# Side work around the seven-part products of an output projection: one VectorE operation per unit, and ScalarE in the making of the scale and bias rows

## The chip, the cores and the metric

The kernel runs on one core of a Trainium2 chip. The metric is the time of one execution on the device, in microseconds (us). The engines are TensorE (PE in the profile, with PEld for its weight loads), VectorE (DVE), ScalarE (ACT), GpSimd (POOL), and the queue of SyncE (SPq) that issues nearly all DMAs. Each engine executes its own list of instructions in order and waits at semaphores for the others.

## The reference, cut to what matters

One layer over 256 frames of width 4096: an input projection, two groups of heads (an attention with forgetting and a linear recurrence), a gate, an output projection, and a LayerNorm of the residual sum:

```python
h = jnp.concatenate([fox_out, rwkv_out], axis=-1) * jax.nn.silu(z.astype(f32))
out = jnp.einsum('bsc,cd->bsd', h.astype(x.dtype), w_out)          # (256, 4096) @ (4096, 4096)
x = _layernorm(ALPHA * x.astype(f32) + out.astype(f32), ln_gain, ln_bias, LN_EPS).astype(x.dtype)
```

Everything is float32. The change touches only the output projection and the preparation of the LayerNorm.

## The kernel before, in words

**Products in three parts.** A float32 operand goes through TensorE as a high part and a low part. ScalarE casts the high part (`split`, line 149), VectorE subtracts it from the operand for the low part (line 150), and TensorE runs three matmuls of 128x512 for each product: high by high, low by high, high by low. The third one is the first that needs VectorE's low part. The low parts stand in a ring of three tiles, the high parts in a ring of four: VectorE can begin a low part when TensorE is through with the tile three before it, ScalarE when it is through with the tile four before.

**The output projection.** The 4096 output columns are eight blocks of 512. `wo{b}_{q}` is the weight tile of block b and rows 256q to 256q+255, two contraction tiles of 128, so a plain tile (kind `n` of the plan) costs 12 matmuls. The two halves of the frames are `oacc_0` and `oacc_1`. The plan, a list of (kind, block, q), sets the order: blocks 0 and 1, then block 2 (q 6 to 11 first, then 0 to 5, then 12 to 15), then blocks 3 and 4 as a pair, then 5 and 6 as a pair, then block 7.

**Units of seven-part products.** In a pair, the rows of q 6 to 11 (`FEW`) go by a scheme with seven products in place of eight for a 2x2 block matrix. One such q is a unit. GpSimd makes four sums of weights (`combine`, kinds `t12` and `t34`, lines 307 to 311, four operations of 128x512 into the tiles `t`), and ScalarE and VectorE split the parts `e1` (1024 columns), `e2` (512 columns), `e3` and `e4` (1024 columns each, from GpSimd's sums). Two plain tiles of the pair are woven into each unit, so a unit is 21 matmuls of parts and 24 of plain tiles, and its six splits come in the order e1, plain, e2, e3, plain, e4.

**Recombined left factors.** The scheme needs sums of the left operand too. For each q in `FEW`, `combine_left` runs six GpSimd operations (lines 1020 to 1025, tile `sf`), and `split_left` splits them on ScalarE and VectorE (lines 1031 and 1032, tiles `sq` and `h`), and then starts the recombination for q+2. The six `split_left` are in the list `todo` when block 2 begins, and the first two recombinations are made ahead of it.

**Side work.** `todo` holds small jobs, and `drain(k)` issues the next k of them at a place of the plan: in block 2 one job at q 0, 1, 3, 5 and 13, in a pair two jobs at each of the first four plain tiles and at those behind the last unit, one at every other plain tile and one at each e4. When a block is complete its results are added into the residual `res` (`add`, lines 1085 and 1087), its statistics are taken (`stats`, BN_STATS, line 1076), and the residual is multiplied by the LayerNorm gain `lg` (`gain`, line 1099). In a pair the inner products are merged first (`merge`, lines 1046 and 1049).

**Scale and bias rows.** At its end the kernel applies the mean and the bias with a matmul against `rows`, six partitions by 4096 columns. `load_tok(b)` makes the part of block b: two DMAs into `rr`, a ScalarE cast to `rh` (line 974), a VectorE product by a constant column to `rt` (line 976), and a VectorE multiply-add into `rows` (line 977). `load_tok` is called once for each block, close to the place where the block begins; the tiles `rr`, `rh` and `rt` have one buffer each.

A scheduler turns this program into one list of instructions for each engine. It may move an instruction ahead of others whose inputs come later, except where `issue_after` or `keep_in_program_order` holds it.

## Time and profile before

| what | us |
|---|---|
| median of 3 runs | 1913.76 (1913.2 to 1914.81) |
| the profiled execution's own time | 1912.92 |
| its span, first to last instruction | 1911.1 |
| PE busy | 1898.2 (99%) |
| DVE busy | 1477.9 (77%) |
| ACT busy | 1009.1 (53%) |
| POOL busy | 404.9 (21%) |

The execution has 1.8 us around its span. The granted TensorE clock was 0.999 of full speed. Matmuls are pipelined in TensorE: the length of one in a row is not its cost; the distance between the starts of two neighbours is. A line number such as L150 is a line of the kernel before; behind the change, lines from 970 on stand 6 to 18 lines lower. In a row of the timeline stand the start, the length, engine, line, operation, out<-in (buffer numbers left out), sizes, and in brackets the idle time ahead of the instruction with what ended it.

### The profile page before, as it was taken

The page shows a single profiled execution, that of the slowest core. Times are in us where ns is not written, and L with a number is a line of the kernel's source. Part 1 is how long each engine was busy: PE and PEld are TensorE (multiplying, and loading weights), DVE is VectorE, ACT ScalarE, POOL GpSimd, SP SyncE. Part 2 cuts the span into 40 slices and gives each one's busy share as a digit, 9 for nine tenths or more (in the row PEclk, how much of TensorE's full clock was granted, in tenths as well). Part 3 has the DMA queues.
Part 4 walks back from the last instruction along what each step waited for, and adds up shares of the span by engine and source line. Part 5 has one row for each costly group of instructions (what it writes and reads, how often), then busy time and mean ns, then how long its engine had stood idle before and what let it go on. Part 6 is the DMA issues. An engine that isn't in the chain of part 4 may idle for free.

```text
span 1911.1 us, 28218 instructions
## 1 busy us (share of the span) xinstructions
PE 1898.2 (99%) x9757; PEld 1576.5 (82%) x9757; DVE 1477.9 (77%) x2417; ACT 1009.1 (53%) x1577; POOL 404.9 (21%) x549
## 2 busy tenths in 40 slices
PE   9999999999999999999999999999999999999998
PEld 9887888888888888888888888888888878877786
DVE  7578868776877687768776877787778775799996
ACT  6554555456545654465446554645464554455443
POOL 0022102200211021002200220022002213386530
PEclk9999999999999999999999999999999999999999
DMA  9668777876777678766876687668767976766665
GB/s 348 181 209 229 199 204 227 232 222 186 231 223 230 186 223 233 227 192 210 235 228 193 208 251 217 195 208 244 216 197 218 308 247 191 234 210 213 204 226 183
DMA packets 272324, 421.37 MB, mean 220 GB/s; under 512 B 142579, under 2 KB 171397, under 8 KB 272181
## 3 DMA queue, kind: packets, MB, share of 16 engines
q1 hardware_dynamic: 271892, 419.23, 72.7%
q8 instruction: 76, 1.25, 0.3%
q14 instruction: 68, 0.55, 0.1%
q10 hardware_dynamic: 288, 0.34, 0.1%
HBM read 389.86 MB, written 29.64 MB: 220 GB/s over the span
## 4 chain that ended last, share of the span: by engine, by line
PE 95%; DVE 2%; POOL 1%; DMA 1%; ACT 0%; issue 0%; SPq 0%; DVEq 0%; ACTq 0%; POOLq 0%
PE acc L155 24%; PE acc L157 24%; PE acc L156 24%; PE oacc L995 5%; PE oacc L992 5%; PE oacc L993 5%; PE rh L738 1%; PE gp L624 1%; PE up L769 1%; PE sp L779 1%; PE accl L157 0%; PE p L993 0%; PE accl L156 0%; PE p L995 0%; PE p L992 0%; PE accl L155 0%
## 5 line engine op out<-in xcount | busy, mean ns | idle before, releaser
L853 POOL COPY pT<-lg 32x96 f32<-32x96 f32 x128 | 57.1, 446 | 633.2 <-DVE lg L849 628.4
L661 POOL COPY BKt<-BK 32x192 f32<-32x192 f32 x128 | 73.7, 576 | 62.5 <-DVE BK L658 57.5
L694 DVE TENSOR_REDUCE xc<-prod 128x8 f32<-128x16 f32 (+30 forms) x248 | 72.7, 293 | 6.6
L691 DVE TENSOR_TENSOR prod<-Nb,xc 128x8 f32<-128x8 f32 (+30 forms) x248 | 72.3, 292 | 3.0
L150 DVE TENSOR_TENSOR w_0l<-w,w_0h 128x1024 fp32r<-128x1024 f32 x31 | 38.4, 1238 | 33.6 <-ACT w_0h L149 25.1
L149 ACT CAST w_0h<-w 128x1024 fp32r<-128x1024 f32 x31 | 32.5, 1048 | 54.9 <-DMA w<-in_w_main_dram 38.0
L149 ACT CAST w_8h<-w 128x1024 fp32r<-128x1024 f32 x31 | 32.6, 1052 | 48.7 <-PE acc L156 17.3
L149 ACT CAST w_6h<-w 128x1024 fp32r<-128x1024 f32 x31 | 32.7, 1055 | 46.9 <-PE acc L156 36.9
L150 DVE TENSOR_TENSOR w_9l<-w,w_9h 128x1024 fp32r<-128x1024 f32 x31 | 38.0, 1226 | 24.7 <-ACT w_9h L149 9.8
L150 DVE TENSOR_TENSOR w_11l<-w,w_11h 128x1024 fp32r<-128x1024 f32 x31 | 37.9, 1223 | 21.8 <-PE acc L157 16.1
L150 DVE TENSOR_TENSOR w_10l<-w,w_10h 128x1024 fp32r<-128x1024 f32 x31 | 37.9, 1223 | 20.4 <-issue 7.9
L150 DVE TENSOR_TENSOR w_15l<-w,w_15h 128x1024 fp32r<-128x1024 f32 x31 | 38.0, 1225 | 18.3 <-issue 12.9
L550 POOL COPY hr<-hr 32x16 f32<-32x16 f32 x64 | 45.7, 715 | 26.8 <-DVE hr L547 24.4
L150 DVE TENSOR_TENSOR w_6l<-w,w_6h 128x1024 fp32r<-128x1024 f32 x31 | 38.9, 1255 | 16.0 <-ACT hry L812 10.3
L149 ACT CAST w_10h<-w 128x1024 fp32r<-128x1024 f32 x31 | 32.6, 1053 | 34.0 <-DMA w<-in_w_main_dram 18.6
L149 ACT CAST w_1h<-w 128x1024 fp32r<-128x1024 f32 x31 | 32.7, 1053 | 33.9 <-DMA w<-in_w_main_dram 21.3
L155 PE MATMUL acc<-w_15h,x 128*128 128x512 f32 x124 | 50.2, 405 | 0.0
L155 PE MATMUL acc<-w_9h,x 128*128 128x512 f32 x124 | 50.0, 403 | 0.0
L157 PE MATMUL acc<-w_12l,x 128*128 128x512 f32 x124 | 48.5, 391 | 1.1 <-DVE w_12l L150 1.1
L150 DVE TENSOR_TENSOR w_7l<-w,w_7h 128x1024 fp32r<-128x1024 f32 x31 | 37.9, 1222 | 15.1 <-PE acc L157 13.1
L155 PE MATMUL acc<-w_14h,x 128*128 128x512 f32 x124 | 49.5, 399 | 0.0
L150 DVE TENSOR_TENSOR w_3l<-w,w_3h 128x1024 fp32r<-128x1024 f32 x31 | 37.8, 1221 | 14.9 <-PE acc L157 14.6
(1031 smaller groups left out, 6896.2 us busy)
## 6 DMA issues: line engine op xcount, KB each, us to landing
w<-in_w_main_dram SPq DMA_DIRECT2D x496, 512.0 KB, 4.1
wo<-in_w_o_dram SPq DMA_DIRECT2D x122, 512.0 KB, 4.6
bt<-bk SPq DMA_DIRECT2D x88, 128.0 KB, 4.2
Nb<-nd SPq DMA_DIRECT2D x16, 512.0 KB
hd<-hl SPq DMA_DIRECT2D x29, 256.0 KB
h<-hd SPq DMA_DIRECT2D x29, 256.0 KB, 6.2
wr<-in_w_first_dram SPq DMA_DIRECT2D x15, 384.0 KB, 6.8
lr<-in_w_lora_dram SPq DMA_DIRECT2D x15, 336.0 KB, 6.6
```

The source lines that it names most:

```text
L149: latest[1] = nc.scalar.copy(hi[:, :n], src[:, :n])
L150: latest[0] = nc.vector.tensor_tensor(lo[:, :n], src[:, :n], hi[:, :n].bitcast(F32), ALU.subtract)
L155: nc.tensor.matmul(acc[:, :n], xs[k][:, 0, tt], hi[:, o : o + n], start=(k == 0), stop=False)
L156: nc.tensor.matmul(acc[:, :n], xs[k][:, 1, tt], hi[:, o : o + n], start=False, stop=False)
L157: nc.tensor.matmul(acc[:, :n], xs[k][:, 0, tt], lo[:, o : o + n], start=False, stop=(k == KT - 1))
L661: nc.gpsimd.tensor_copy(BKt[B * b : B * (b + 1), :, :, B * a : B * (a + 1)], BK[B * a : B * (a + 1), :, : NCH - 1, B * b : B * (b + 1)])
L691: first = nc.vector.tensor_tensor(prod[:, :, :, s + 1 :], nb[:, :, s : s + 1, s + 1 :].to_broadcast([P, 2, NJ, w]), xc[:, :, :, s + 1 :], ...
L694: solved = nc.vector.tensor_reduce(xc[:, :, :, s : s + 1], prod[:, :, :, s:], AX.X, ALU.add)
L853: (nc.gpsimd.tensor_copy if b % 2 else nc.scalar.copy)(pT[B * b : B * (b + 1), :, B * a : B * (a + 1)], lg[B * a : B * (a + 1), :, B * b : ...
L992: nc.tensor.matmul(acc, h, hi, start=n[0] == n[1], stop=False)
L993: nc.tensor.matmul(acc, l, hi, start=False, stop=False)
L995: nc.tensor.matmul(acc, h, lo, start=False, stop=not n[0])
```

## The change

The row making leaves `load_tok` for a function of its own, `load_rows`, in which ScalarE makes `rt` as well as `rh`, tied behind the latest weight cast; the last step, into `rows`, becomes a job. For blocks 0 and 1 it is issued at the old place; those for blocks 2 to 7 are started in block 2, at every second tile, each put at the head of `todo`. Block 2's places for jobs become a table, `before_2`. In a pair, a unit gets one job, at its first plain tile, in place of up to three; the first two plain tiles of the first pair get none.

```diff
@@ load_tok
         nc.sync.dma_start(out=lgain[b], in_=lng[:, o].to_broadcast([P, OB]))
+        if b < 2:
+            load_rows(b)()
+
+    def load_rows(b):
+        o = slice(b * OB, (b + 1) * OB)
         rr = rpool.tile([6, OB], F32, tag="rr", name=f"rr{b}")
         nc.sync.dma_start(out=rr[0:3], in_=lng[:, o].to_broadcast([3, OB]))
         nc.sync.dma_start(out=rr[3:6], in_=lnb[:, o].to_broadcast([3, OB]))
         rh = rpool.tile([6, OB], F32R, tag="rh", name=f"rh{b}")
-        nc.scalar.copy(rh, rr)
         rt_ = rpool.tile([6, OB], F32, tag="rt", name=f"rt{b}")
-        nc.vector.tensor_scalar(rt_, rh.bitcast(F32), cs[0:6, C_ROW : C_ROW + 1], None, ALU.mult)
-        nc.vector.scalar_tensor_tensor(rows[0:6, o], rr, cs[0:6, C_ROW + 1 : C_ROW + 2], rt_, ALU.mult, ALU.add)
+        with tc.issue_after(latest[1].ins):
+            nc.scalar.copy(rh, rr)
+            nc.scalar.mul(rt_, rh.bitcast(F32), cs[0:6, C_ROW : C_ROW + 1])
+        return lambda: nc.vector.scalar_tensor_tensor(rows[0:6, o], rr, cs[0:6, C_ROW + 1 : C_ROW + 2], rt_, ALU.mult, ALU.add)
@@ before the loop over the plan
     count = {3: 0, 5: 0}
+    plan_2 = [q for _, b, q in plan if b == 2]
+    before_2 = {2: 1, 4: 1, 6: 1, 7: 1, 8: 2, 9: 1, 10: 1, 11: 1, 12: 1, 13: 1, 15: 1}
     whole = len(FEW) * 6 + LEAD
@@ in the loop
-            drain((2 if n <= LEAD or n > whole else 1) if kind == "n" else kind == "e4")
-        elif b > 1:
-            drain(2 if b == NB - 1 else q in (0, 1, 3, 5, 13))
+            apart_ = kind == "n" and (n <= LEAD or n > whole)
+            if apart_ and (pair > 3 or n > 2):
+                drain(1 if (pair, n) == (3, LEAD) else 2)
+            elif not apart_ and (n - LEAD) % 6 == 5:
+                drain(1)
+        elif b == NB - 1:
+            drain(2)
+        elif b == 2:
+            turn_ = plan_2.index(q)
+            if turn_ in before_2:
+                drain(before_2[turn_])
+            if turn_ % 2 == 0 and turn_ < 12:
+                todo.insert(0, load_rows(2 + turn_ // 2))
```

TensorE's list is the same before and after. VectorE's loses the eight `rt` products, ScalarE's gains them. What the scheduler makes of the rest is shown at three places.

**VectorE, second half of block 2.** `wo_5l` and the like are low parts of weight tiles, `sq` and `h` a recombined left factor, and a row that writes `rows` is the last step of the row making. Before:

```order
L150 TENSOR_TENSOR wo_12l<-wo_12_16061,wo_12h 128x1024
L976 TENSOR_SCALAR rt_16497<-rh_16495,cs 6x512
L977 SCALAR_TENSOR_TENSOR rows<-rr_16492,cs,rt_16497 6x512
L150 TENSOR_TENSOR wo_13l<-wo_13_16091,wo_13h 128x1024
L1032 TENSOR_TENSOR sq_16145<-sf_16042,sq_16145 128x384
L1032 TENSOR_TENSOR h_14895<-sf_16042,h_14895 128x128
L150 TENSOR_TENSOR wo_14l<-wo_14_16121,wo_14h 128x1024
L976 TENSOR_SCALAR rt_16993<-rh_16991,cs 6x512
L977 SCALAR_TENSOR_TENSOR rows<-rr_16988,cs,rt_16993 6x512
L150 TENSOR_TENSOR wo_15l<-wo_15_16139,wo_15h 128x1024
```

After:

```order
L150 TENSOR_TENSOR wo_5l<-wo_5_16050,wo_5h 128x1024
L983 SCALAR_TENSOR_TENSOR rows<-rr_16031,cs,rt_16035 6x512
L150 TENSOR_TENSOR wo_12l<-wo_12_16069,wo_12h 128x1024
L1038 TENSOR_TENSOR sq_16147<-sf_16080,sq_16147 128x384
L1038 TENSOR_TENSOR h_14854<-sf_16080,h_14854 128x128
L150 TENSOR_TENSOR wo_13l<-wo_13_16122,wo_13h 128x1024
L983 SCALAR_TENSOR_TENSOR rows<-rr_16099,cs,rt_16103 6x512
L150 TENSOR_TENSOR wo_14l<-wo_14_16141,wo_14h 128x1024
L1038 TENSOR_TENSOR sq_16203<-sf_16092,sq_16203 128x384
L1038 TENSOR_TENSOR h_14895<-sf_16092,h_14895 128x128
L150 TENSOR_TENSOR wo_15l<-wo_15_16178,wo_15h 128x1024
```

The `rows` steps stand at other tiles, and the split of the third recombined factor (its `h` is `h_14854`), which stood ahead of `wo_12l`, now stands behind it. Ahead of the rows shown, the first two splits moved from behind `wo_2l` and `wo_3l` to behind `wo_4l`, one after the other.

**ScalarE at the same place.** `rh` and `rt` are the first two steps of the row making. Before:

```order
L149 CAST wo_13h<-wo_13_16091 128x1024
L1031 CAST sq_16145<-sf_16042 128x384
L1031 CAST h_14895<-sf_16042 128x128
L974 CAST rh_16495<-rr_16492 6x512
L149 CAST wo_14h<-wo_14_16121 128x1024
L149 CAST wo_15h<-wo_15_16139 128x1024
```

After:

```order
L981 CAST rh_16034<-rr_16031 6x512
L1037 CAST sq_16147<-sf_16080 128x384
L982 ACTIVATE rt_16035<-rh_16034,cs 6x512
L1037 CAST h_14854<-sf_16080 128x128
L149 CAST wo_13h<-wo_13_16122 128x1024
L149 CAST wo_14h<-wo_14_16141 128x1024
L1037 CAST sq_16203<-sf_16092 128x384
L981 CAST rh_16102<-rr_16099 6x512
L1037 CAST h_14895<-sf_16092 128x128
L982 ACTIVATE rt_16103<-rh_16102,cs 6x512
L149 CAST wo_15h<-wo_15_16178 128x1024
```

An `rt` now stands behind an `sq`, the cast that waits for GpSimd's recombination, and the `rows` step of VectorE that uses it stands ahead of the next low part.

**VectorE in the first pair, from the second unit's first plain tile.** `e_3_8l` is a part of the third unit (q 8). Before:

```order
L150 TENSOR_TENSOR wo_1l<-wo_1_16430,wo_1h 128x1024
L150 TENSOR_TENSOR e_3_7l<-t_3_7_16407,e_3_7h 128x1024
L150 TENSOR_TENSOR e_3_8l<-wo_8_16426,e_3_8h 128x1024
```

After:

```order
L150 TENSOR_TENSOR wo_1l<-wo_1_16460,wo_1h 128x1024
L150 TENSOR_TENSOR e_3_7l<-t_3_7_16436,e_3_7h 128x1024
L150 TENSOR_TENSOR e_3_8l<-wo_8_16456,e_3_8h 128x1024
L1105 TENSOR_TENSOR res_15796<-res_15796,lg_16108 128x512
L150 TENSOR_TENSOR wo_12l<-wo_12_16472,wo_12h 128x1024
```

Before, the last side operation of the first pair's units stands in the first unit (two additions, two BN_STATS and two gains around q 6). Now the two additions and one BN_STATS stand there, the other BN_STATS in the second unit, and one gain each in the third and the fourth. In the second pair, the two gains that stood in the first unit and at the head of the second now stand in the third and the fourth.

## The prediction

> **What bounds the kernel now.** I read the page's head first.

> ```profile
> span 1911.1 us, 28218 instructions
> PE 1898.2 (99%) x9757; PEld 1576.5 (82%) x9757; DVE 1477.9 (77%) x2417; ACT 1009.1 (53%) x1577; POOL 404.9 (21%) x549
> ```

> TensorE is busy for 99% of the span and sets the end, and its list of matmuls does not change. So only the moments count in which it waits. The starts in its timeline show them:

> ```profile
> 1674.74 0.39 PE L992 MATMUL oacc<-wo_14h,h 128*128 128x512 f32 x1
> ...
> 1677.46 0.39 PE L992 MATMUL oacc<-wo_15h,hl 128*128 128x512 f32 x1
> 1677.68 0.39 PE L993 MATMUL oacc<-wo_15h,hl 128*128 128x512 f32 x1
> 1678.60 0.50 PE L995 MATMUL oacc<-wo_15l,hl 128*128 128x512 f32 x1 [0.53 <-DVE wo_15l L150]
> ...
> 1691.88 0.39 PE L992 MATMUL p<-e_6h,h 128*128 128x512 f32 x1
> ...
> 1747.98 0.50 PE L995 MATMUL oacc<-wo_15l,hl 128*128 128x512 f32 x1
> ...
> 1778.36 0.39 PE L992 MATMUL p<-e_6h,h 128*128 128x512 f32 x1
> ...
> 1833.74 0.50 PE L995 MATMUL oacc<-wo_15l,hl 128*128 128x512 f32 x1
> ```

> A tile of 12 matmuls takes 1677.46-1674.74 = 2.72, so the pitch is 0.227. The step of 0.92 before 1678.60 has 0.7 of waiting in it, and 0.1 more in refilling: block 2 loses 0.8. From the first part of the first unit to the waiting matmul of the last there are five units of 45 and eight more, 233 matmuls or 52.8. The first pair took 56.1 (loses 3.3), the second 55.4 (loses 2.6). That is 6.7 us to be had in all, 0.35%.

> Why the units lose shows in VectorE's and GpSimd's timelines of one unit:

> ```profile
> 1713.53 2.32 DVE L150 TENSOR_TENSOR wo_12l<-wo,wo_12h 128x1024 fp32r<-128x1024 f32 x1
> 1715.78 1.78 DVE L150 TENSOR_TENSOR e_8l<-res,e_8h 128x512 fp32r<-128x512 f32 x1
> ...
> 1718.61 1.21 DVE L150 TENSOR_TENSOR wo_2l<-wo,wo_2h 128x1024 fp32r<-128x1024 f32 x1
> ...
> 1724.23 2.32 DVE L150 TENSOR_TENSOR wo_13l<-wo,wo_13h 128x1024 fp32r<-128x1024 f32 x1
> 1723.18 2.28 POOL L310 TENSOR_TENSOR t<-wo 128x512 f32<-128x512 f32 x1
> 1700.00:1750.00 50.00, 49.60 (x213) 39.24 (x212) 50.00 (x29) 26.72 (x28) 40.33 (x19) 1.00 0.55 195
> ```

> The same split takes 1.21 (start to start 1.14) or 2.32: beside a GpSimd operation VectorE stands still for 1.1. The last row is the table of stretches (length; busy PE, PEld, DVE, ACT, POOL): VectorE is busy for all 50 us. A unit costs it five splits of 1.14, one of 0.6 and four holds of 1.1 = 10.7, as wo_12l to wo_13l shows; TensorE needs 45x0.227 = 10.2. So a unit loses 0.5 **with no side operation at all**, and the third to the sixth had none.

> What a side operation costs beside GpSimd:

> ```profile
> 1688.47 3.46 POOL L310 TENSOR_TENSOR t<-res,res 128x512 f32<-128x512 f32 x1
> 1690.27 0.68 DVE L1076 BATCH_NORM_STATS2 lst<-res 128x6 f32<-128x512 f32 x1
> 1690.88 1.60 DVE L1099 TENSOR_TENSOR res<-res,lg 128x512 f32<-128x512 f32 x1
> ```

> BN_STATS takes its usual 0.68 while GpSimd's operation runs, and fits inside a hold. The gain waits until that operation ends: it costs 0.6 of its own and admits a hold of 1.1 ahead of the split behind it. [...]

> **First term: block 2's start, +0.3** (0 to +0.7).

> ```profile
> 1641.11 1.22 DVE L150 TENSOR_TENSOR wo_8l<-wo,wo_8h 128x1024 fp32r<-128x1024 f32 x1
> 1642.51 0.40 PE L995 MATMUL oacc<-wo_8l,h 128*128 128x512 f32 x1
> L977 DVE SCALAR_TENSOR_TENSOR rows<-rr,cs,rt x8: 723/798/1112, 1623.0 to 1688.5; 6x512 fp32r<-6x512 f32 x8
> L976 DVE TENSOR_SCALAR rt<-rh,cs x8: 468/733/1055, 1622.5 to 1685.3; 6x512 f32<-6x512 f32 x8
> ```

> wo_8l is ready 0.18 ahead of its matmul. Block 1's `rows` step (at least 0.72) now stands behind wo_7l; in exchange rt and rows leave the place ahead of block 0's additions, but these can move forward only to where TensorE is done with block 0, some 0.3. 0.7-0.3-0.18 = 0.2, with the refill 0.3.

> **Second term: the loop of four engines in block 2, +1.0** (-0.8 to +3.1). Eight rt products of about 0.73 (5.9 us) leave VectorE; ScalarE gets them for about the 0.62 of its `rh` below, hidden, as it is busy for 27 of 50 in the stretch above. That is not the price. The price is what `rows` now waits for:

> ```profile
> 1655.21 0.74 POOL L1020 TENSOR_TENSOR sf<-h 128x256 f32<-128x256 f32 x1 [28.60 <-DVE h L1032]
> 1662.96 0.74 POOL L1020 TENSOR_TENSOR sf<-h 128x256 f32<-128x256 f32 x1
> 1667.65 0.74 POOL L1020 TENSOR_TENSOR sf<-h 128x256 f32<-128x256 f32 x1
> 1670.18 3.73 POOL L1023 TENSOR_TENSOR sf<-sf 128x128 f32<-128x128 f32 x1
> 1674.40 0.74 POOL L1020 TENSOR_TENSOR sf<-h 128x256 f32<-128x256 f32 x1
> 1680.76 0.53 POOL L1025 TENSOR_TENSOR sf<-sf 128x128 f32<-128x128 f32 x1
> 1659.11 1.21 DVE L150 TENSOR_TENSOR wo_4l<-wo,wo_4h 128x1024 fp32r<-128x1024 f32 x1
> 1669.81 0.83 DVE L977 SCALAR_TENSOR_TENSOR rows<-rr,cs,rt 6x512 fp32r<-6x512 f32 x1
> 1670.57 1.20 DVE L150 TENSOR_TENSOR wo_13l<-wo,wo_13h 128x1024 fp32r<-128x1024 f32 x1
> 1672.38 1.21 DVE L150 TENSOR_TENSOR wo_14l<-wo,wo_14h 128x1024 fp32r<-128x1024 f32 x1
> 1674.47 0.52 ACT L1031 CAST sq<-sf 128x384 fp32r<-128x384 f32 x1 [3.61 <-POOL sf L1025]
> 1675.09 0.62 ACT L974 CAST rh<-rr 6x512 fp32r<-6x512 f32 x1
> 1675.74 0.80 DVE L976 TENSOR_SCALAR rt<-rh,cs 6x512 f32<-6x512 f32 x1 [2.16 <-ACT rh L974]
> 1677.34 1.21 DVE L150 TENSOR_TENSOR wo_15l<-wo,wo_15h 128x1024 fp32r<-128x1024 f32 x1
> ```

> GpSimd makes four recombinations without a break, in 7.8, 4.7, 6.8 and 6.9. The second has 4.7; the third lost 3.3 to one operation of some 0.4 that began beside `rows` (1670.18) and came to an end only behind wo_14l, when VectorE fell idle: VectorE's run shuts GpSimd out. Behind a recombination stand, in a line, ScalarE's sq, then rh, then VectorE's rt, rows and the low part of the next tile: from 1674.40 to 1678.55, 4.1 us. That is the 0.8 lost in block 2 today.

> Now the first recombination begins behind wo_4l instead of wo_2l: two tiles or 5.4 later, at 1660.6. The first takes about 4.9, since VectorE falls idle behind wo_5l (its `rows` waits for this very recombination): 1665.5. The second meets `rows`, wo_12l, sq, h, wo_13l in a run and is shut out: 7, 1672.5. Behind it stand sq, rh, h, rt on ScalarE, then rows and wo_14l on VectorE, 4.1 by the line above: 1676.6. TensorE needs wo_14l at 1674.74+0.45 = 1675.2: loss 1.4. The third is shut out again, until 1679.5; then sq and h (0.8), the cast of wo_0 (1.05) and its low part (1.2): 1682.5, where TensorE, late by 1.4, needs it at 1682.0: 0.4 more. The fourth finds slack. Loss 1.8 for 0.8: +1.0. I take this middle as it uses each row at its nearest place. Low end: no loss (-0.8). High end: the four as slow as before on average, 26.1 in all, which puts wo_2l, behind the fourth, at 1660.6+26.1+3.3 = 1690.0, needed at 1677.46+3x2.72+0.45 = 1686.1: loss 3.9.

> **Third term: the units of the first pair, -0.7** (-1.8 to +0.3).

> ```profile
> 1794.08 1.54 DVE L150 TENSOR_TENSOR wo_1l<-wo,wo_1h 128x1024 fp32r<-128x1024 f32 x1 [0.97 <-issue]
> 1798.91 2.32 DVE L150 TENSOR_TENSOR wo_12l<-wo,wo_12h 128x1024 fp32r<-128x1024 f32 x1
> ```

> Five side operations in and just ahead of the first unit are gone (rt, rows, a BN_STATS, two gains). So VectorE enters the second unit with the ring full, and begins the second plain tile there (wo_1l) when TensorE leaves wo_5, some 0.2 behind it. From wo_1l's start to wo_12l's end are 7.15 in the second pair. The new gain ahead of wo_12l adds 0.6 and lets a hold of 1.1 in: 8.85. TensorE needs wo_12l 35 matmuls or 7.9 after leaving wo_5: 8.85+0.2-7.9, or 1.2, lost. The next unit, again with a gain, costs 11.3 against 10.2: 1.1, with slips 1.3. In the fifth the hold, which the gain had moved ahead, is not paid twice, and in the sixth 0.1 is lost. Together 2.6 for 3.3. Ends: VectorE arrives late as before (+0.3), or half of the holds fall into its idle time as one does ahead of wo_1l (1.5 lost, -1.8).

> **Fourth term: the second pair, 0** (-1.1 to +0.3). The gain that stood ahead of wo_5l and lost about 1 there is gone, but the same 2.6 comes back behind the two later gains. Work on VectorE that is only moved within a saturated stretch ends at the same moment.

> At nothing I cost: the 16 small DMAs of `rr`, which are as many as before and stand in SPq among weight loads that already wait for `rows` without TensorE waiting (row below); the later loads of `lg`, half a pair ahead of use; and the end, where the same instructions come in a slightly other order and VectorE has about 2 us in hand.

> ```profile
> SPq L971 <- DVE rows L977: 10.7, 5, 3.9
> ```

> **Sum**: +0.3+1.0-0.7+0 = +0.6. The profiled execution's 1912.92 becomes 1913.5; it stands 0.84 below the median of the runs, so against the median 1914.4.

> **Rivals.** (1) *GpSimd is not shut out*: it keeps its turn, recombinations take 4.7 each, the second ends at 1670.0, wo_14l is ready in time, block 2 loses nothing; with the pairs at their low ends (1.5 lost in each) the sum is +0.3-0.8-1.8-1.1 = -3.4, 1910.4. For it: the second recombination, and GpSimd's regular turns in the units. Against: 1670.18 and two more like it. [...] The row shows the waiting operation passed over by four.
> (2) *The loop closes*: slower. With recombinations of 6.5 on average the second term is +3.1 and the sum +2.7; from 6.8 on it passes +3.8; at 7.8, the worst row, wo_2l is ready at 1695.1, 9.0 late, and the sum is +7.8: 1921.6. For it: three of four rows were 6.8 or more. Against: `rows` stands beside two of the four now, and VectorE has gaps.
> (3) *The change doesn't do what it says*: units 5 and 6 have no side operation and two others a gain that is no cheaper than before, so units gain nothing: +1.3, 1915.1. This lies in my range.

> **Chances.** Forecast with its neighbourhood (-1.5 to +2.6) and rival 3: 0.60; rival 1: 0.22, half of it beyond -0.2%; rival 2: 0.18, 0.14 of it beyond +0.2%. A measurement of this kernel tells about 0.2% (3.8 us) from no change. So faster 0.11, within 0.75, slower 0.14. The range reaches into both rivals: 1910.8 to 1918.0.

> **What would show it.** Right: TensorE waits at wo_14l and wo_0l of block 2, behind VectorE idle for ScalarE's rt, behind sq for GpSimd; waits of about 1 at wo_12l and wo_13l of each pair; none at wo_0l and wo_5l there. Wrong: 233 matmuls of a pair in under 54.5 us, or recombinations above 6.8.

## The result, and the profile after

| kernel | median us (runs) | lowest to highest | ratio to before, 95% interval |
|---|---|---|---|
| before | 1913.33 (22) | 1911.98 to 1914.81 | |
| changed | 1916.81 (22) | 1915.50 to 1918.19 | 1.0019, 1.0012 to 1.0025 |

The change makes the kernel slower, by 3.5 us. The forecast was 1914.4, a sum of +0.6 on the profiled execution. The direction and the range hold, the size doesn't. The head of the profile after reads as before, with 0.9 us more of TensorE and 9 us less of VectorE:

```profile
span 1915.6 us, 28227 instructions
PE 1899.1 (99%) x9757; PEld 1579.4 (82%) x9757; DVE 1468.6 (77%) x2409; ACT 1013.7 (53%) x1585; POOL 390.8 (20%) x549
```

The changed kernel's TensorE timeline, at the places that the prediction counts (start, length, operation, idle time ahead of it and what ended it):

```profile
1676.38 0.50 PE L1001 MATMUL oacc<-wo_14l,h 128*128 128x512 f32 x1 [0.20 <-DVE wo_14l L150]
...
1682.35 0.50 PE L1001 MATMUL oacc<-wo_0l,h 128*128 128x512 f32 x1 [0.23 <-DVE wo_0l L150]
...
1689.32 0.50 PE L1001 MATMUL oacc<-wo_2l,h 128*128 128x512 f32 x1 [1.24 <-DVE wo_2l L150]
...
1694.46 0.39 PE L998 MATMUL p<-e_6h,h 128*128 128x512 f32 x1
...
1751.60 0.44 PE L1001 MATMUL oacc<-wo_15l,hl 128*128 128x512 f32 x1
...
1781.93 0.39 PE L998 MATMUL p<-e_6h,h 128*128 128x512 f32 x1
...
1805.80 0.50 PE L1001 MATMUL oacc<-wo_12l,h 128*128 128x512 f32 x1 [1.29 <-DVE wo_12l L150]
...
1817.35 0.50 PE L1001 MATMUL oacc<-wo_13l,h 128*128 128x512 f32 x1 [0.93 <-DVE wo_13l L150]
...
1838.17 0.50 PE L1001 MATMUL oacc<-wo_15l,hl 128*128 128x512 f32 x1
```

With the prediction's measure, time between two starts less 0.2267 for each matmul, three stretches can be compared: block 2 (216 matmuls, from wo_8's first to the first part of the pair), and 233 matmuls of each pair. The same table takes in the experiments below; where a kernel ran beside the kernel before on the same chip, the last column is its median less that one's.

| kernel | block 2 | first pair | second pair | sum | sum less before | median less before |
|---|---|---|---|---|---|---|
| before | 0.9 | 3.3 | 2.6 | 6.7 | | |
| changed | 2.6 | 4.3 | 3.4 | 10.3 | +3.6 | +3.5 |
| changed, run again | 2.6 | 4.3 | 3.4 | 10.3 | +3.6 | +3.5 |
| block-2 half alone | 2.6 | 1.9 | 2.4 | 6.9 | +0.2 | +0.4 |
| pair half alone | 1.2 | 3.9 | 3.8 | 8.9 | +2.2 | +1.8 |
| BN_STATS for gains | 2.6 | 2.0 | 1.5 | 6.1 | -0.6 | -0.6 |
| rows apart | 0.0 | 3.7 | 3.8 | 7.4 | +0.7 | +1.1 |
| no jobs in units | 0.0 | 2.0 | 1.5 | 3.4 | -3.3 | -0.7 |
| rows apart, old pairs | 0.0 | 1.5 | 2.5 | 4.0 | -2.7 | -1.9 |
| the same again | 0.0 | 1.5 | 2.5 | 4.0 | -2.7 | -2.0 |
| last gain behind | 0.0 | 1.5 | 1.5 | 3.0 | -3.7 | -2.7 |

The sum of the three stretches (+3.6) and the medians (+3.5) agree, so the changed kernel's loss is in these stretches. The two traced spans differ by 4.5. The other 0.9 stands ahead of block 2, which begins at 1642.9 in the changed kernel's trace and at 1642.1 in that of the kernel before, and anywhere from 1641.8 to 1643.7 in the traces of the experiments (but the one that adds long reductions).

**Block 2** waits at wo_14l and wo_0l, as the prediction says, but most of it at wo_2l. The chain there, from the timelines of VectorE, ScalarE and GpSimd (L983 writes `rows`, L982 makes `rt`, L1037 and L1038 are `sq` and `h`, L1026 to L1031 the recombination):

```profile
1668.54 3.87 POOL L1031 TENSOR_TENSOR sf<-sf 128x128 f32<-128x128 f32 x1
1672.45 0.52 ACT L1037 CAST sq<-sf 128x384 fp32r<-128x384 f32 x1 [1.98 <-POOL sf L1031]
1673.59 0.72 ACT L982 ACTIVATE rt<-rh,cs 6x512 f32<-6x512 f32 x1
1674.34 0.85 DVE L983 SCALAR_TENSOR_TENSOR rows<-rr,cs,rt 6x512 fp32r<-6x512 f32 x1 [2.25 <-ACT rt L982]
1674.73 3.73 POOL L1029 TENSOR_TENSOR sf<-sf 128x128 f32<-128x128 f32 x1
1685.11 1.29 POOL L307 TENSOR_TENSOR t<-res,wo 128x512 f32<-128x512 f32 x1
1685.17 0.52 ACT L1037 CAST sq<-sf 128x384 fp32r<-128x384 f32 x1 [2.39 <-POOL sf L1031]
1685.72 1.09 DVE L1038 TENSOR_TENSOR sq<-sf,sq 128x384 fp32r<-128x384 f32 x1 [0.91 <-ACT sq L1037]
1686.74 1.39 DVE L1038 TENSOR_TENSOR h<-sf,h 128x128 fp32r<-128x128 f32 x1
1688.05 1.21 DVE L150 TENSOR_TENSOR wo_2l<-wo,wo_2h 128x1024 fp32r<-128x1024 f32 x1
```

VectorE stands idle for `rt`, which stands behind `sq` on ScalarE, which waits for GpSimd, where the last operation of the recombination took 3.87; others of its shape take 0.46. Then VectorE's next run keeps another of them from ending for 3.73. The last recombination ends at 1685.1, and behind it stand the cast of wo_2 on ScalarE and `sq` and `h` on VectorE. These two, 0.54 and 0.27 at 1676.3, take 1.09 and 1.39 there, beside the sums of the first unit, which GpSimd began at 1685.1.

**The first pair** loses 1.9 at wo_12l, behind a gain, and then something that no line of the program contains. (By the condition `(n - LEAD) % 6 == 5` the job of a unit is issued at the unit's second plain tile, not at its first; in VectorE's list it lands ahead of the next unit's first plain tile.) The first five rows are VectorE and GpSimd, the others TensorE, then the table of stretches (length; busy PE, PEld, DVE, ACT, POOL; granted clock; DMA share and rate):

```profile
1712.65 2.31 DVE L150 TENSOR_TENSOR e_8l<-wo,e_8h 128x1024 fp32r<-128x1024 f32 x1
1714.89 1.78 DVE L1105 TENSOR_TENSOR res<-res,lg 128x512 f32<-128x512 f32 x1
1716.59 2.30 DVE L150 TENSOR_TENSOR wo_12l<-wo,wo_12h 128x1024 fp32r<-128x1024 f32 x1
1713.84 2.28 POOL L310 TENSOR_TENSOR t<-res,res 128x512 f32<-128x512 f32 x1
1716.08 1.73 POOL L311 TENSOR_TENSOR t<-wo,t 128x512 f32<-128x512 f32 x1
1718.94 0.50 PE L1001 MATMUL oacc<-wo_12l,h 128*128 128x512 f32 x1 [1.78 <-DVE wo_12l L150]
1719.98 0.53 PE L998 MATMUL oacc<-wo_12h,h 128*128 128x512 f32 x1
...
1723.28 0.49 PE L1001 MATMUL oacc<-e_8l,sq 128*128 128x512 f32 x1
1716.69:1720.10 3.41, 1.63 (x8) 1.03 (x7) 3.41 (x3) 1.04 (x1) 1.12 (x1) 1.00 0.67 163
1720.10:1723.51 3.41, 3.41 (x10) 2.67 (x9) 1.31 (x2) 1.04 (x1) 2.55 (x2) 0.50 0.79 289
```

From 1719.98 on, one microsecond after the wait is over, the matmuls' starts stand 0.32 apart once and then 0.42 to 0.43, in place of 0.227, for 3.3 us in all, and the granted clock is 0.50. The eight steps from 1719.98 to 1723.28 take 3.30 for 1.81, so 1.5 are lost there. Busy time doesn't show it: PE is busy for all of that last stretch.

### The profile page after: what moved, and what is told of

Read it like the earlier page. It is cut to its first block, busy times and chain, and to the rows that moved or that the text cites. A ratio compares the mean times of both kernels' runs of the same rounds, so it can differ in the third digit from the quotient of the medians.

```text
span 1915.6 us, 28227 instructions
## 1 busy us (share of the span) xinstructions
PE 1899.1 (99%) x9757; PEld 1579.4 (82%) x9757; DVE 1468.6 (77%) x2409; ACT 1013.7 (53%) x1585; POOL 390.8 (20%) x549
## 4 chain that ended last, share of the span: by engine, by line
PE 95%; DVE 2%; POOL 1%; DMA 0%; ACT 0%; issue 0%; SPq 0%; DVEq 0%; ACTq 0%; POOLq 0%
PE acc L155 24%; PE acc L157 24%; PE acc L156 23%; PE oacc L1001 5%; PE oacc L998 5%; PE oacc L999 5%; PE rh L738 1%; PE gp L624 1%; PE up L769 1%; PE p L999 1%; PE p L1001 1%; PE p L998 1%; PE sp L779 1%; PE accl L155 1%; PE accl L156 1%; PE accl L157 1%
## 5 line engine op out<-in xcount | busy, mean ns | idle before, releaser
L150 DVE TENSOR_TENSOR w_0l<-w,w_0h 128x1024 fp32r<-128x1024 f32 x31 | 38.2, 1231 | 32.3 <-ACT w_0h L149 24.2
L149 ACT CAST w_6h<-w 128x1024 fp32r<-128x1024 f32 x31 | 32.7, 1055 | 46.8 <-PE acc L156 36.8
L150 DVE TENSOR_TENSOR w_9l<-w,w_9h 128x1024 fp32r<-128x1024 f32 x31 | 38.0, 1226 | 24.8 <-ACT w_9h L149 12.7
L150 DVE TENSOR_TENSOR w_10l<-w,w_10h 128x1024 fp32r<-128x1024 f32 x31 | 37.9, 1224 | 22.9 <-ACT w_10h L149 8.8
L150 DVE TENSOR_TENSOR w_11l<-w,w_11h 128x1024 fp32r<-128x1024 f32 x31 | 37.9, 1222 | 20.7 <-PE acc L157 14.6
L150 DVE TENSOR_TENSOR w_6l<-w,w_6h 128x1024 fp32r<-128x1024 f32 x31 | 39.9, 1288 | 16.0 <-ACT hry L812 10.3
L150 DVE TENSOR_TENSOR w_15l<-w,w_15h 128x1024 fp32r<-128x1024 f32 x31 | 38.0, 1227 | 16.9 <-issue 15.4
L150 DVE TENSOR_TENSOR w_7l<-w,w_7h 128x1024 fp32r<-128x1024 f32 x31 | 37.9, 1222 | 15.1 <-PE acc L157 13.1
L150 DVE TENSOR_TENSOR w_3l<-w,w_3h 128x1024 fp32r<-128x1024 f32 x31 | 37.8, 1220 | 14.9 <-PE acc L157 14.6
L155 PE MATMUL acc<-w_1h,x 128*128 128x512 f32 x124 | 49.2, 397 | 0.0
```

Source lines behind the costliest of these rows:

```text
L149: latest[1] = nc.scalar.copy(hi[:, :n], src[:, :n])
L150: latest[0] = nc.vector.tensor_tensor(lo[:, :n], src[:, :n], hi[:, :n].bitcast(F32), ALU.subtract)
L155: nc.tensor.matmul(acc[:, :n], xs[k][:, 0, tt], hi[:, o : o + n], start=(k == 0), stop=False)
```

## The experiments

The first theory: two separable parts, block 2's loop (1.7 by the table) and the gains in the third and fourth unit (the rest, with the half clock in it). The rivals: one part alone is the cause; any operation in a unit costs alike; the half clock is chance.

### The block-2 half alone

The changed kernel, with the pairs' job places of before.

```diff
-            apart_ = kind == "n" and (n <= LEAD or n > whole)
-            if apart_ and (pair > 3 or n > 2):
-                drain(1 if (pair, n) == (3, LEAD) else 2)
-            elif not apart_ and (n - LEAD) % 6 == 5:
-                drain(1)
+            drain((2 if n <= LEAD or n > whole else 1) if kind == "n" else kind == "e4")
```

> The block-2 half of the change alone: row making by ScalarE and the table of places of block 2 stay, the pairs get the job places of the kernel before. Theory (two separable parts: the loop of four engines in block 2 costs 1.8 us, the gains in the third and fourth unit cost the rest): 1913.3 + 1.8 = 1915.1, with block 2 losing about 2.6 at wo_14l, wo_0l and wo_2l, and no half clock in the first pair, since no TensorE wait there exceeds 1.3. Rival A (the pairs alone make it slower; what block 2 loses is given back by the lead that the pair then has): 1913.3 to 1913.8. Rival B (block 2 is the whole cause, also of the pair's losses): 1916.8, with the waits at wo_12l of the first pair still there.

Measured: 1913.69, ratio 1.0003 (0.9994 to 1.0012). Rival A's time: block 2 loses its 2.6, and the first pair gives 1.3 of the 1.7 back. The rows of VectorE and GpSimd at the pair's start show by what:

```profile
1693.51 1.28 DVE L1105 TENSOR_TENSOR res<-res,lg 128x512 f32<-128x512 f32 x2
...
1690.06 2.38 POOL L311 TENSOR_TENSOR t<-wo,t 128x512 f32<-128x512 f32 x1
1697.80 1.29 POOL L307 TENSOR_TENSOR t<-wo,wo 128x512 f32<-128x512 f32 x1 [5.37 <-DVE e_6l L150]
```

VectorE, late by block 2's waits, comes to block 2's two gains at 1693.51, when GpSimd has ended its first sums (1690.06 + 2.38) and has not begun the next (1697.80). Both together take 1.28. In the kernel before they stand beside GpSimd and take 1.60 and 1.77. So the two parts aren't separable, and the part that writes the rows costs almost nothing by itself: alone the two halves lose 0.2 and 2.2 by the sums of the table, together 3.6.

### The pair half alone

The kernel before, with the changed pairs; the split that block 2 of the kernel before leaves over goes to the pair's first tile.

```diff
-            drain((2 if n <= LEAD or n > whole else 1) if kind == "n" else kind == "e4")
+            apart_ = kind == "n" and (n <= LEAD or n > whole)
+            if apart_ and (pair > 3 or n > 2):
+                drain(1 if (pair, n) == (3, LEAD) else 2)
+            elif apart_ and n == 1:
+                drain(1)
+            elif not apart_ and (n - LEAD) % 6 == 5:
+                drain(1)
```

> The pair half alone: block 2 and the row making as before, the pairs with one job per unit (the sixth recombined factor's split, which block 2 of the kernel before leaves over, is issued at the first tile of the first pair). Theory: waits of 1 to 2 us at wo_12l of both pairs behind the gain ahead of it, about 1 at wo_13l; +0.3 by waits in the first pair, +0.8 in the second, and 1.5 more if the wait at wo_12l is again long enough to halve the clock: 1914.4 without, 1915.9 with it. Rival A (pairs alone are the cause): 1916.8. Rival B (block 2 is the whole cause): 1912.6 to 1913.3, since two gains leave the first unit.

Measured: 1915.06, ratio 1.0010 (1.0002 to 1.0019). Slower by itself, without a half clock in its trace, and between what the theory (1914.4) and Rival A (1916.8) gave; Rival B (1912.6 to 1913.3) falls. The pairs lose 0.6 and 1.2 more than before. Block 2, which this kernel leaves as it was, loses 0.4 more in this trace, at wo_8l, which was ready only 0.18 ahead in the kernel before. The gain and its wait in the first pair:

```profile
1713.97 1.79 DVE L1099 TENSOR_TENSOR res<-res,lg 128x512 f32<-128x512 f32 x1
...
1718.04 0.50 PE L995 MATMUL oacc<-wo_12l,h 128*128 128x512 f32 x1 [1.55 <-DVE wo_12l L150]
1729.61 0.50 PE L995 MATMUL oacc<-wo_13l,h 128*128 128x512 f32 x1 [0.97 <-DVE wo_13l L150]
```

Here both waits come, at wo_12l and at wo_13l. In the changed kernel wo_13l is ready 0.25 ahead, because VectorE gained time while TensorE ran at half clock. So of the 1.5 that the half clock takes, about 1.1 stands in place of the wait at wo_13l.

### BN_STATS in place of the gains

The changed kernel, with one more BN_STATS of the same tile wherever a gain stands in a unit; these four multiplications are left out.

```diff
+        if in_unit:
+            return stats(m, b)
         nc.vector.tensor_tensor(res[m][:, o], ..., lgain[b], ALU.mult)
...
+                in_unit = True
                 drain(1)
+                in_unit = False
```

> The changed kernel in which each gain inside a unit (two in each pair) is replaced by one more BN_STATS of the same tile; these four multiplications by the gain are left out. Theory (an operation with two SBUF inputs waits for GpSimd and lets one hold of 1.1 more in, one with a single input slips into a hold): the waits at wo_12l and wo_13l fall to 0.3 or less, no half clock, the first pair loses 2.6 in place of 4.3 and the second 2.6 in place of 3.4: 1916.8 - 2.5 = 1914.3. Rival (any operation in a unit costs VectorE its own time plus a hold, since VectorE is saturated there): 1916.3 to 1916.8, waits as in the changed kernel.

Measured: 1912.69, ratio 0.9997 (0.9988 to 1.0006), 4.1 under the changed kernel, where 2.5 was expected. The same place as above, VectorE and TensorE:

```profile
1715.68 0.69 DVE L1082 BATCH_NORM_STATS2 lst<-res 128x6 f32<-128x512 f32 x1
1716.29 1.71 DVE L150 TENSOR_TENSOR wo_12l<-wo,wo_12h 128x1024 fp32r<-128x1024 f32 x1
...
1718.05 0.50 PE L1001 MATMUL oacc<-wo_12l,h 128*128 128x512 f32 x1
```

An operation with one input, at the very place of the gain, ends in 0.69, and the hold of the split behind it shrinks from 1.1 to 0.5. The pairs lose 2.0 and 1.5, as much as with no job in the units at all (below): it costs nothing. The rival falls. But BN_STATS also writes far less than a gain (128x6 for 128x512). An addition of a block's results tells the two apart: it has the shape of a gain, and its second input comes from TensorE's accumulators (PSUM) in place of SBUF. In the kernel before:

```profile
1681.25 4.69 POOL L307 TENSOR_TENSOR t<-res,wo 128x512 f32<-128x512 f32 x1
1684.70 0.67 DVE L1087 SCALAR_TENSOR_TENSOR res<-res,oacc 128x512 f32<-128x512 f32 x1
```

It takes 0.67 while GpSimd's operation runs; the gains in that kernel's first unit took 1.60 and 1.77, and the four in the changed kernel's units take 1.77 or 1.78 each. So by these rows what makes the changed kernel slow in the pairs is the second SBUF input of those four gains.

### Rows apart

Rows of blocks 2 to 4 at tiles 0, 2 and 4 of block 2, those of blocks 5 to 7 in block 7, the splits of the recombined factors alone in the second half of block 2.

```diff
-    before_2 = {2: 1, 4: 1, 6: 1, 7: 1, 8: 2, 9: 1, 10: 1, 11: 1, 12: 1, 13: 1, 15: 1}
+    before_2 = {2: 1, 4: 1, 6: 1, 7: 1, 8: 1, 9: 1, 11: 1, 13: 1, 15: 1}
...
         elif b == NB - 1:
             drain(2)
+            if q in (0, 2, 4):
+                todo.insert(0, load_rows(5 + q // 2))
...
-            if turn_ % 2 == 0 and turn_ < 12:
+            if turn_ % 2 == 0 and turn_ < 6:
```

> The changed kernel with the rows of blocks 2 to 4 started at tiles 0, 2 and 4 of block 2, ahead of any recombined factor's split, and those of blocks 5 to 7 at tiles 0, 2 and 4 of block 7; the six splits alone at tiles 7, 8, 9, 11, 13 and 15 of block 2. Theory (the loss in block 2 is rows that wait behind a recombination, and recombinations shut out beside rows): recombinations of 5.5 or less on average, VectorE never idle for rt behind sq, block 2 loses 0.8 or less in place of 2.6: 1916.8 - 1.8 = 1915.0, or 1913.5 if a better lead into the first pair also shortens the wait at wo_12l under the length that halves the clock. Rival (the recombinations are shut out by the low parts and the splits themselves, whatever the rows do): block 2 loses 2 or more, 1916.3 to 1916.8. Against it a second one: the rows in block 7 delay the low parts there, +0.5.

Measured: 1914.39, ratio 1.0006 (0.9997 to 1.0015); block 2 loses nothing at all. Groups of VectorE from 1655 to 1692, first of the changed kernel, then of this one (count; busy, mean ns; idle time ahead and what ended it):

```profile
L1038 DVE TENSOR_TENSOR sq<-sf,sq 128x384 fp32r<-128x384 f32 x6 | 3.8, 639 | 2.4 <-ACT sq L1037 2.4
L983 DVE SCALAR_TENSOR_TENSOR rows<-rr,cs,rt 6x512 fp32r<-6x512 f32 x4 | 3.2, 798 | 7.1 <-ACT rt L982 7.1
```

```profile
L1038 DVE TENSOR_TENSOR sq<-sf,sq 128x384 fp32r<-128x384 f32 x6 | 4.4, 737 | 6.3 <-ACT sq L1037 6.3
L983 DVE SCALAR_TENSOR_TENSOR rows<-rr,cs,rt 6x512 fp32r<-6x512 f32 x1 | 0.7, 733 | 0.0
```

VectorE waits 6.3 for ScalarE's `sq` and `rt` in place of 9.5, and no row stands behind a recombination any more. GpSimd's four recombinations take 22.3 in this stretch in place of 24.0, so 5.6 each for 6.0, a little over the 5.5 of the expectation. None of their operations takes over 1.8, where the changed kernel has 3.87 and 3.73. The fourth recombination ends 39.0 after block 2's first matmul in place of 42.2, because the first one begins 1.9 earlier (its split no longer stands behind a row) and the four, from the first start to the last end, are shorter by 1.3. So it is the rows' places that lose the 2.6 in block 2; how much of that is VectorE idle for `rt` and how much the later recombinations, this run does not separate. The pairs keep their waits (1.7 and 1.1 in the first, 1.5 and 1.4 in the second), and there is no half clock. Block 7 takes no longer (77.4 from the second pair's wo_15l to the span's end, in both kernels), so the +0.5 of the second rival doesn't come.

### What halves the clock

The kernel before, with one long reduction of VectorE in every second block of the input projection (one execution, 1942.7).

```diff
+    idle6 = const.tile([P, 16], F32, name="idle6")
...
+            if b % 2 == 0 and q == 8:
+                long_ = 8 + n
+                with tc.issue_after(latest[0].ins):
+                    tc.keep_in_program_order(nc.vector.tensor_reduce(idle6[:, :long_], ..., AX.X, ALU.add))
```

> The kernel before, with one idle reduction of VectorE in every second block of the input projection (128 partitions, 8x512 to 15x512 elements, so some 4 to 8 us each; its result is not used), fixed between two low parts. TensorE then waits at 15 places, from nothing to about 3 us, at 15 different phases. Only what the granted clock does behind each wait is looked at, not the kernel's time. Theory (the wait at wo_12l of the changed kernel is what halved the clock): behind waits of up to 1.7 the pitch stays at 0.227, behind waits from about 1.9 on eight or so matmuls run at 0.427, some 3.4 us after the wait began. Rival A (a matter of chance or of load elsewhere): half clock at some places without regard to the wait, or at none. Rival B (the share of the wait in a fixed window counts, so the phase matters): between 1.5 and 3 some waits halve the clock and others of the same length don't.

Two waits (TensorE's timeline), then the table of stretches around these and a third, cut into cells of 3.41:

```profile
1313.89 1.22 PE L157 MATMUL acc<-w_12l,x 128*128 128x512 f32 x2 [2.76 <-DVE w_12l L150]
...
1510.06 0.74 PE L157 MATMUL acc<-w_12l,x 128*128 128x512 f32 x2 [3.26 <-DVE w_12l L150]
```

```profile
1310.40:1313.81 3.41, 0.73 (x4) 0.27 (x2) 3.37 (x6) 1.04 (x1) 0.00 (x0) 0.99 0.43 98
1313.81:1317.22 3.41, 3.33 (x8) 2.65 (x9) 3.22 (x5) 0.00 (x0) 1.17 (x1) 0.51 0.97 249
1504.92:1508.33 3.41, 1.88 (x9) 1.22 (x7) 3.34 (x6) 1.04 (x1) 0.00 (x0) 1.00 0.57 165
1508.33:1511.75 3.42, 1.69 (x7) 1.42 (x8) 3.42 (x5) 0.00 (x0) 0.00 (x0) 1.00 0.54 138
733.50:736.91 3.41, 1.69 (x8) 1.42 (x8) 3.41 (x5) 1.00 (x1) 0.00 (x0) 1.00 0.48 120
736.91:740.32 3.41, 3.41 (x16) 2.81 (x16) 2.59 (x3) 0.00 (x0) 2.84 (x3) 1.00 1.01 268
```

Rival B is right: the wait of 2.76 halved the clock, the longer one of 3.26 didn't. Of the eight long waits of this trace, 5.51 and 2.76 halved it; 3.26, 2.22 and four of 1.69 to 1.72 didn't. Where it halved, half clock began 2.9 after the wait did in the changed kernel (1717.16 to 1720.08) and 2.7 behind the 2.76 here (1311.13 to 1313.8), for the theory's 3.4. The changed kernel's trace gives the length of a cell: its granted clock is 0.50 from 1720.08 to 1723.50, so for 3.41, is whole behind that, and falls to 0.50 again at 1911.23, behind the last matmul. From 1723.50 to there are 187.73, which is 55 times 3.413. Two half-clock stretches of the run with the reductions end at 160.1 and 1317.2, 339 times 3.413 apart, and the stretches above are cut by that grid, to within 0.1. The wait of 2.76 leaves 0.73 of work in one cell, and the next cell runs at 0.51. The wait of 3.26 falls across a boundary and leaves 1.88 and 1.69 in its two cells: full clock. A wait of 1.72 that lies wholly in a cell (at 735.23) leaves 1.69: full clock. In the changed kernel 1.63 is left, cut to fit its half-clock stretch, and the next 3.41 run at 0.50; the cell ahead of the drop at 1911.23 has 1.15. In rows apart and the pair half alone, the cells with the waits at wo_12l of the first pair keep about 1.9 of work (3.41 less 1.51 and 1.55 of idle time), and the clock stays whole (1.000 in both profiled executions). In the cells looked at, work of 1.69 or more never led to half clock, and work of 1.63 or less always did. The length of a wait alone doesn't decide it: 1.78 was enough in the changed kernel, and 3.26 was harmless here.

### The changed kernel again

No edit.

> The changed kernel once more, unaltered. If the half clock behind wo_12l of the first pair belongs to this kernel, the new trace shows it again, with a wait of 1.7 to 2.0 ahead of it, and the time is 1916.8 again. If it was a chance of one execution, the new trace has the wait but the full clock, and the first pair loses 2.8 in place of 4.3.

Measured: 1916.72, ratio 1.0018 (1.0009 to 1.0027). The half clock is there again, in a new execution, behind a wait of 1.80 at the same matmul, so it isn't a chance of one trace. It doesn't come in every execution. Such a stretch takes 1.7 us of full clock off a span of 1914, so the mean granted clock of its execution is 0.999 or less; two of the first 22 executions of the changed kernel have 1.000, and their times, 1916.15 and 1916.70, are near the median of 1916.81. So the kernel is about as slow without it. This fits the grid, if a wait falls into it by chance: one of 1.78 halves the clock only where it lies wholly in a cell, which by these lengths is about half of the places it can take (an estimate: 3.41 less 1.78, of 3.41).

### No jobs in the units

Rows apart, and:

```diff
-                drain(1 if (pair, n) == (3, LEAD) else 2)
-            elif not apart_ and (n - LEAD) % 6 == 5:
-                drain(1)
+                drain(3 if pair > 3 and n in (2, 3) else 2)
```

> Rows apart, as in the kernel with the rows in blocks 2 and 7, and no job in any unit: the two gains of block 2 go behind the last unit of the first pair, two tiles of the second pair's lead take three jobs in place of two, and what is left over goes behind the second pair's last unit. Theory (VectorE needs 10.7 for a unit that takes TensorE 10.2, so a pair that starts with a full ring loses only what the ring doesn't cover): block 2 loses 0, the first pair 1.0 to 1.5, the second 1.0 to 1.5, in all 2.5 for 6.7: 1913.3 - 4.2 = 1909.1; 1 more if the later jobs push block 7's low parts back. Rival (five units lose 0.5 each whatever the ring holds at their start): pairs of 2.5 each, 1911.6.

Measured: 1912.47, ratio 0.9995 (0.9986 to 1.0004). The second pair does as expected (1.5), the first less well (2.0), and 2.1 is lost behind the pairs: from wo_15l of the second pair to the span's end are 79.5 here and 77.4 in the kernel before. The four jobs that the second pair's units no longer take are too much for block 7, where the three rows alone cost nothing (rows apart). The largest wait there is 1.02, at wo_13l of block 7.

### Rows apart, with the old pairs

The edit of "Rows apart" and that of "The block-2 half alone" together.

> Rows apart, with the pairs' job places of the kernel before (gains of block 2 at the first pair's lead, gains of the second pair in its first unit). Theory: block 2 loses 0, the first pair 2 to 2.6, since its lead is not spent on rows any more, the second 2.5 as before: 4.8 for 6.7, 1911.4. Rival (what block 2 doesn't lose, the first pair loses, as it was the other way round with the changed block 2 alone): 1913.0 to 1913.3.

Measured: 1911.31, ratio 0.9990 (0.9981 to 0.9999). Block 2 keeps its full gain of 0.9, and the first pair loses 1.5 for 3.3: the rival (the pair takes back what block 2 saves) falls. Behind the pairs 0.4 is lost (77.8 from wo_15l of the second pair to the end, for 77.4), a part of what the stretches show more than the median does.

### The last gain behind the units

In that kernel, no job in the second pair's units after the first unit's first plain tile; in VectorE's list the last gain then stands ahead of wo_0l, that unit's second plain tile.

```diff
-            drain((2 if n <= LEAD or n > whole else 1) if kind == "n" else kind == "e4")
+            if kind == "n" and (n <= LEAD or n > whole):
+                drain(2)
+            elif pair == 3 or n == LEAD + 2:
+                drain(1 if kind == "n" else kind == "e4")
```

> The kernel with rows apart and the old pairs' places, but in the second pair no job from the second unit's first split on: one gain (the one that took 1.78 beside GpSimd ahead of wo_5l) goes behind the last unit. Theory: the wait of 0.93 at wo_5l is gone, the second pair loses 1.5 to 1.8 in place of 2.5, block 7 loses 0 to 0.4 for one job more: 0.5 to 1.0 under that kernel, 1910.6. Rival (VectorE is saturated in the units, so the same loss comes back at the later units): no change, 1911.3.

> The kernel with rows apart and the pairs' job places of the kernel before once more, beside the one above on the same chip: 1911.3, under the kernel before by 1.5 to 2.5. If the gain was chance, 1913.

Measured, on one chip: 1910.37, ratio 0.9984 (0.9975 to 0.9992), and for the kernel without this edit 1911.14, 0.9992 (0.9983 to 1.0001). The step between the two, 0.8, is within the medians' uncertainty. The traces show it directly: the wait at wo_5l is gone, and the second pair loses 1.5 in place of 2.5. This version beats the kernel before by 2.7 us, and so the changed kernel by some 6.2 (2.7 and 3.5, each against the kernel before).

## Why the prediction was off, step by step

The time lies in the stated range, and the change made the kernel slower as forecast, but this is partly luck: the range reached into both rivals, and two of the four terms lie outside their own bounds.

**Block 2's start, +0.3.** Nothing is lost. wo_8l is ready 0.42 ahead of its matmul:

```profile
1641.76 1.20 DVE L150 TENSOR_TENSOR wo_8l<-wo,wo_8h 128x1024 fp32r<-128x1024 f32 x1
1643.38 0.39 PE L1001 MATMUL oacc<-wo_8l,h 128*128 128x512 f32 x1
```

**The loop in block 2, +1.0.** It is +1.7, inside its bounds, and the loop is the one described. Two of its places were named rightly: wo_0l loses the forecast 0.4, wo_14l 0.4 in place of 1.4, since the second recombination ended 5.2 behind the first where the forecast had 7. The step that failed is "The fourth finds slack": it sets wo_2l back by 1.4. Recombinations took 5.8, 5.2, 6.6 and 6.2 (the forecast had 4.9, 7 and 7), on average under the second rival's 6.5.

**The sum of terms.** A second, larger fault is that this term was added to the next one. Late work of VectorE in block 2 met GpSimd elsewhere, and the gains behind it became cheap: 1.3 came back in the first pair, and the block-2 half alone is +0.4 by the median. The changed kernel doesn't get this back, because its pair half takes those gains out of the cheap place.

**The first pair, -0.7.** It is +1.0, outside its bounds. The step that failed is "So VectorE enters the second unit with the ring full", and with it the 7.15 from wo_1l's start to wo_12l's end. Both were taken from the second pair, which has a lead of 4.4 at its start. The changed first pair comes out of a wait at wo_2l, and most of its low parts are ready only 0.1 to 1.2 ahead in the first unit. So VectorE has no idle time ahead of wo_1l, where it had 0.97 in the second pair's row, and one hold more falls on its work: e_8l takes 2.31 (in the rows above) for 1.21. The starts of wo_1l in the first pair, changed kernel first, before second:

```profile
1709.27 1.21 DVE L150 TENSOR_TENSOR wo_1l<-wo,wo_1h 128x1024 fp32r<-128x1024 f32 x1
1707.92 1.21 DVE L150 TENSOR_TENSOR wo_1l<-wo,wo_1h 128x1024 fp32r<-128x1024 f32 x1
```

In the kernel before it is 7.9 from there to the end of wo_12l (1713.53 + 2.32); with the gain's 1.7 this makes the 9.6 of the changed kernel, where the forecast had 8.85. So 1.9 is lost at wo_12l, for 1.2. Then the clock halves, which no step had. It takes 1.5 and removes the forecast wait of 1.1 at wo_13l, so its net price is about 0.4.

**The second pair, 0.** It is +0.9, also outside. The waits stand where the prediction put them, at wo_12l and wo_13l, and none at wo_5l. The step that failed is "Work on VectorE that is only moved within a saturated stretch ends at the same moment". The stretches of the second pair, changed kernel first, before second:

```profile
1781.93:1838.17 56.24, 54.02 (x235) 43.36 (x233) 50.88 (x34) 30.42 (x32) 37.51 (x20) 1.00 0.53 173
```

```profile
1778.36:1833.74 55.38, 54.40 (x234) 43.33 (x232) 52.27 (x33) 30.65 (x32) 40.99 (x20) 1.00 0.51 173
```

VectorE is idle for 5.4 us of the changed stretch and for 3.1 of the one before: it isn't saturated. Behind each long wait of TensorE it stands still, since the ring of three low parts comes free only as TensorE goes on (wo_2l waits 1.0 so, behind the wait at wo_12l). What a gain costs depends on the lead of the low part just ahead of it, the time from its end to its first use. A gain and the held split behind it take VectorE 3.9, and TensorE's six matmuls between the first uses of the two low parts take 1.4. With 0.1 from the end of a low part to its matmul, the wait is 2.6 less the lead. In the first unit of the second pair of the kernel before that low part has a lead of 1.7, and the gain costs 0.9. In the changed kernel's third unit it has 1.2, and it costs 1.5; in the fourth 1.6, and it costs 1.1; in the third unit of the first pair 0.7, and it costs 1.9. In all 19 places of the traces where TensorE waits behind a gain and a held split, lead and cost together are 2.6; behind the half clock the lead is 2.8, and the gain costs nothing.

**What held.** BN_STATS in a unit costs nothing, as the row of 0.68 said; the gain costs its own time and a hold. A unit without a side operation loses something, but 0.3 to 0.4 in place of 0.5: a wait of 0.2 to 0.3 and 0.1 of refilling (the step behind a wait is 0.33 to 0.34, for 0.227), as at wo_13l, wo_14l and wo_15l of most kernels here. No wait is at wo_0l or wo_5l of the pairs. The first rival is out, since GpSimd is shut out twice in block 2 (3.87 and 3.73 for 0.46). The second rival has the right side, but its reason, the loop, gives only 1.7 of the 3.6; 1.9 is lost in the pairs.

## What to carry to other kernels

Price an operation of VectorE by its number of SBUF inputs and by what GpSimd does at that moment, and then compare it with the lead of the buffer ring at that very place; beside GpSimd an operation with one (BN_STATS, an addition) took 0.67 or 0.68 here, the same gain, with two, took 0.64 by itself or 1.78 beside it, and cost TensorE between nothing and 1.9, by the lead of the low part ahead of it. Do not add the losses of two neighbouring stretches as if they were independent: a wait moves all later work against the other engines, and may return most of its price (1.3 of 1.7 here). Keep work that waits for a slow producer (rows behind a recombination) out of the queue on which the bounding engine's operands are made: block 2 lost 2.6 with the rows there and nothing with the rows apart.
